# Other places in SBUF for the matmul operands of a two-block float32 network

## The chip, the cores and the metric

The kernel runs on one core of a Trainium2 chip. The metric is the device time of one execution in microseconds (us); durations of single instructions are in nanoseconds (ns). All inputs and outputs are float32.

## The reference, cut to what matters

The input is one sequence of 256 tokens of 1024 channels. A first network of two layers and a second of two layers run one after the other. Cut to its matrix products:

```python
def swiglu(h, w_gate, w_up, w_down):                     # 1024 -> 2816 -> 1024
    return (silu(h @ w_gate) * (h @ w_up)) @ w_down
# first block: swiglu, even mixer, swiglu, swiglu, odd mixer, swiglu
for layer in range(2):                                   # second block
    proj = h @ w_in[layer]                               # 1024 -> 11776
    y_a, y_b, y_c = retention(proj), hgrn(proj), window_attention(proj)
    merged = sum(sigmoid(gate_i) * (y_i @ w_i) for i in "abc")
    h = layer_norm(alpha * h + merged @ w_o[layer])
    ff = swiglu(h) if layer == 0 else moe(h)             # 8 experts of 3584, 2 per token
    h = layer_norm(alpha * h + ff)
```

The mixers hold small pieces of other work (attention, scans, spatial gates), which take little of the time.

## The kernel before, in words

**Precision.** A float32 operand is split into a high part, rounded to the TensorE's fp32r type, and the rest (`xh`, `xl` for activations, `wh`, `wl` for weights). A product is three fp32r matmuls: high by high, high by low, low by high (`mm3w`, `mm3x`). Everything goes through `mm` (L241), whose second argument is the stationary operand, loaded into the array by a weight load (PEld in the profile), and whose third is the moving operand, streamed through it. In a profile row such as `pa<-xh,wh` the moving operand stands first and the stationary one second.

**Weight stream.** `Stream` reads all weights from HBM in order, in chunks of 128 x 2048 (1 MB, 8192 bytes of each partition), into the tiles `raw` (four buffers, and seven more in the pool `extra` for the experts). Each half chunk is split: ScalarE writes `wh` (L159), VectorE writes `wl` (L160), four buffers each. The loads are issued by SyncE in order; one waits until VectorE has split the chunk that had the buffer before.

**Dense products, weights stationary.** `proj_t_steps` gives the result transposed: the stationary operand is a 128 x 128 piece of the weights (512 bytes of each partition), the moving operand 256 tokens of an activation tile (1024 bytes). Every matmul has a weight load of its own. The moving tiles are `xh`, `xl` (the normed input of each stage), `hh`, `hl` (the hidden layer of a swiglu, `ffn_core`), `oh`, `ol` (in the second block, under this name also `sh`, `hh`, `rh` and the last), and in the mixers `ah`, `gh`, `yh`, `ch` with their low parts. A swiglu runs 22 blocks of gate and up (moving `xh`, `xl`: 22 x 8 x 2 x 3 = 1056 matmuls), then four pairs of output blocks over 22 rows (moving `hh`, `hl`: 4 x 22 x 2 x 3 = 528 matmuls).

**Products with the weights moving.** `proj_x_steps` and the experts: the moving operand is 512 columns of a weight piece (2048 bytes), the stationary one 128 tokens of an activation tile. For an expert these are the gathered tokens `gxh`, `gxl` (`gate_up`) and the hidden layer `mhh`, `mhl` (`down`); expert by expert, seven blocks of 512 hidden columns, with gate and up of a block ahead of the down product of the block before. Gathering (every second expert) and scattering (each expert) are small matmuls between.

**Places in SBUF.** Pools are laid out in the order in which they are opened, tiles in a pool in the order in which they are first used, each right behind the one before. So the place of a tile follows from the sizes ahead of it. The pool `one` (`vecs2` 256 bytes, `x` 8192, the identity and the ones 512 each, `mhalf` 64, `xh` and `xl` 8192 each) begins at byte 16,512 of each partition, which is 128 in its stretch of 512 bytes. Behind it lie `raw`, `hi`, `lo` and `wk`, all multiples of 512 bytes up to `hi` and `lo`. With one stretch meaning 512 bytes, the operands start at these places in a stretch; all their slices lie whole stretches further (for `wh`, `wl`: 512 or 1024 bytes), so the place holds for each matmul:

| operand | before | after |
|---|---|---|
| `wh`, `wl` (stationary in dense products, moving in the experts) | 448 | 448 |
| `xh`, `xl` | 448 | 128 |
| `hh`, `hl` of the first swiglu, `ffn1(0, 0)` | 288 | 128 |
| `hh`, `hl` of `ffn1(0, 1)`, `ffn1(1, 0)` and `ffn2` | 0 | 128 |
| `hh`, `hl` of `ffn1(1, 1)` | 128 | 128 |
| `oh`, `ol` in `layer0` / `layer1` | 0 / 320 | 128 / 128 |
| `ah`, `gh`, `yh`, `ch` with low parts | 32, 224, 192, 192 | 128 |
| `gxh`, `gxl`, `mhh`, `mhl` (the experts' stationary operands) | 320 | 256 |
| `raw` of the pool `raw` / of `extra` | 448 / 480 | 128 / 160 |

Of the kernel before, what the change touches and what calls it, by code (L numbers as in the profile page):

```python
# [9 lines left out]
F32 = mybir.dt.float32  # L10
# [10 lines left out]
KD = D // 128  # L21
# [3 lines left out]
NE = 8  # L25
# [10 lines left out]
N_RAW, N_EXTRA = 4, 7  # L36
# [138 lines left out]
        return self.hi[q][:, o:o + w], self.lo[q][:, o:o + w]  # L175


class Net:
    def __init__(self, ctx, tc, a, consts):
        self.tc, self.nc, self.a = tc, tc.nc, a  # L180
        self.ctx = ctx
        self.cn = consts
        pool = lambda n, b, **k: ctx.enter_context(tc.tile_pool(name=n, bufs=b, **k))
        self.one = pool("one", 1)
        self.raw_p, self.hi_p, self.lo_p = pool("raw", N_RAW), pool("hi", 4), pool("lo", 4)
        self.wk = pool("wk", 2)
        self.pa = pool("pa", 4, space=PSUM)
        self.pb = pool("pb", 4, space=PSUM)
        self.ws = Stream(tc, a["dense"], (self.raw_p, self.hi_p, self.lo_p))
# [25 lines left out]
    def setup(self):  # L215
        nc = self.nc
        self.ctx1 = self.ctx.enter_context(ExitStack())
        one1 = self.ctx1.enter_context(self.tc.tile_pool(name="one1", bufs=1, reuse_waits="tile"))
        self.vecs = {v: p.tile([128, NVEC[v]], F32, name=v) for v, p in (("vecs1", one1), ("vecs2", self.one))}
        nc.scalar.dma_start(self.vecs["vecs1"], self.a["vecs1"])  # L220
        self.x = self.one.tile([128, KD, S], F32, name="x")
        self.ws.load_to(0, [lambda s=slice(2 * d, 2 * d + 2): nc.sync.dma_start(self.x[:, s], self.a["xt"][:, s])
                            for d in range(4)])
        self.ws.split_to(1)
        self.ws.load_to(1)
        self.ident = self.consts(self.one, "all")["ident"]
        nc.gpsimd.dma_start(self.vecs["vecs2"], self.a["vecs2"])
        self.ones = self.one.tile([128, 128], F32, name="ones")
        nc.vector.memset(self.ones, 1.0)
        self.mhalf = self.one.tile([128, 16], F32, name="mhalf")  # L230
        nc.vector.memset(self.mhalf, -0.5)
        self.xh = self.one.tile([128, KD, S], F32R, name="xh")
        self.xl = self.one.tile([128, KD, S], F32R, name="xl")
# [136 lines left out]
        return factors  # L370


    def ffn_core(self, gname, uname, dname, gi, di, factors, done, fill=iter(())):

        nc = self.nc
        with self.tc.tile_pool(name="ffn", bufs=1, reuse_waits="tile") as fp:
            hh = fp.tile([128, NF, S], F32R, name="hh")
            hl = fp.tile([128, NF, S], F32R, name="hl")
            proj = lambda f: self.proj_t([(gname, gi, f * 128, 128), (uname, gi, f * 128, 128)], self.xh, self.xl)
            first = []  # L380
            if factors:
                first = [proj(0), proj(1)]
                rc, R = factors()
            for f in range(NF):
                b = first.pop(0) if first else proj(f)
                sg = self.wk.tile([128, S], F32, name="sg", tag="t256", bufs=4)
                h = self.wk.tile([128, S], F32, name="h", tag="t256", bufs=4)
                if not factors:
                    nc.scalar.activation(sg, b[:, 0], AF.Silu)
                    nc.vector.tensor_mul(h, sg, b[:, 1])  # L390
                else:
                    gu = self.wk.tile([128, 2, S], F32, name="gu", tag="t512", bufs=4)
                    nc.vector.tensor_mul(gu, b, R[:, None, :].to_broadcast([128, 2, S]))
                    nc.scalar.activation(sg, gu[:, 0], AF.Silu)
                    nc.vector.tensor_mul(h, sg, gu[:, 1])
                self.split(hh[:, f], hl[:, f], h)
                if f % 3 == 2:
                    next(fill, None)
            for d in range(KD // 2):
                done(d, lambda: self.proj_t([(dname, di, d * 256, 256)], hh, hl, NF))  # L400
                next(fill, None)

    def ffn1(self, l, j, fill=iter(()), after=None):
        nc = self.nc
        factors = self.rms_in(self.vec("norm", (l * 3 + 2 * j) * 8, 8))

# [3 lines left out]
            if after:  # L410
                after(d)

        self.ffn_core("ffn_w_gate", "ffn_w_up", "ffn_w_down", (l, j), (l, j), factors, done, fill)

    def add_out(self, d, b):
        xp = self.x[:, 2 * d:2 * d + 2]
# [34 lines left out]
    def even(self):  # L451
# [5 lines left out]
        with tc.tile_pool(name="ev", bufs=1, reuse_waits="tile") as P:  # L457
# [60 lines left out]
                nc.scalar.activation(vt[:, t], o[t], AF.Copy, scale=rc[:, t:t + 1])  # L518


            ah = P.tile([128, 4, S], F32R, name="ah")
            al = P.tile([128, 4, S], F32R, name="al")
            tr = nc.tensor.transpose
# [99 lines left out]
            nc.vector.tensor_reduce(ms[:, 1], vq, axis=AX.X, op=OP.add)  # L623
            rv = self.rstd_cols(ms[:, 1], 16, 1.0 / 64, 1e-5)
            nc.vector.tensor_mul(vg, vg, rv[:, :, None].to_broadcast([128, 16, 64]))
            gh = P.tile([128, 4, S], F32R, name="gh")
            gl = P.tile([128, 4, S], F32R, name="gl")
            for i in range(2):
# [141 lines left out]
    def odd(self):  # L770
        nc, W, tc, s5 = self.nc, self.wk, self.tc, self.s5
        factors = self.rms_in(self.vec("norm", 32, 8))
        w, idx = "od_w_in", (0,)
        with tc.tile_pool(name="od", bufs=1, reuse_waits="tile") as P:
            pm = self.consts(P, "odd")["pool"]
            pw = self.load(P, "pw", [128, 4, 128], self.a["pw"])
            u = P.tile([128, 4, S], F32, name="s5u")
# [525 lines left out]

    def moe_fetch(self):

        p = self.ctx2.enter_context(self.tc.tile_pool(name="extra", bufs=N_EXTRA, side="right", reuse_waits="tile"))
        self.moe_ws = Stream(self.tc, self.a["moe"], (self.raw_p, self.hi_p, self.lo_p), extra=p)
        for c in range(N_RAW, N_RAW + N_EXTRA):
# [18 lines left out]
    def router_parts(self):  # L1327

        V = self.nc.vector
        self.wg = self.mo.tile([128, KD, NE], F32, name="wg")  # L1330
        self.wsum = self.mo.tile([128, 2, NE], F32, name="wsum")
        wr, wb = (self.wk.tile([128, KD, NE], F32, name=n, tag="t256", bufs=4) for n in ("wr", "wb"))
        self.nc.gpsimd.dma_start(wr, self.a["router"])
        b = self.pbank((128, 2, NE))
# [29 lines left out]
        self.ln_finish(self.vec("lnmix", 0, 8), self.vec("lnmix", 8, 8))  # L1364

    def ffn2(self):
        self.ffn_core("ffn_w_gate_2", "ffn_w_up_2", "ffn_w_down_2", (0,), (0,), None, self.residual2)
        self.ln_finish(self.vec("lnffn", 0, 8), self.vec("lnffn", 8, 8))

    def ln_stats(self, x):  # L1370
# [35 lines left out]
    def moe(self):  # L1406
# [2 lines left out]
        Z = self.mo  # L1409
        x = self.hx  # L1410
        C = self.consts(Z, "moe")
        cr = Z.tile([128, 2, 128], F32R, name="cr")
        V.tensor_copy(cr[:, 0], C["before"])
        V.tensor_copy(cr[:, 1], self.ones)
# [299 lines left out]
    def run(self):  # L1714
        tc = self.tc
        self.setup()
        with tc.tile_pool(name="evw", bufs=1, reuse_waits="tile") as P:
            steps = self.even_loads(P)
            self.ffn1(0, 0, steps)
            for _ in steps:  # L1720
                pass
            self.even()
        with tc.tile_pool(name="s5p", bufs=1, reuse_waits="tile") as P2:
            with tc.tile_pool(name="s5q", bufs=1, reuse_waits="tile") as P:
                steps = self.s5_params(P, P2)
                self.ffn1(0, 1, steps)
                self.ffn1(1, 0, steps)
                for _ in steps:
                    pass
            self.odd()  # L1730
# [1 line left out]
        self.ctx1.close()  # L1732
        with tc.tile_pool(name="l2", bufs=1, reuse_waits="tile") as Q:
            self.l2 = Q
            self.layer0()
        self.ffn2()
        self.run_last()

    def run_last(self):

        tc = self.tc
        with ExitStack() as self.ctx2:
            self.mo = self.ctx2.enter_context(tc.tile_pool(name="hxp", bufs=1))
            with tc.tile_pool(name="l2b", bufs=1, reuse_waits="tile") as Q:
                self.l2 = Q
                self.layer1()
            self.mo = self.ctx2.enter_context(tc.tile_pool(name="mo", bufs=1, reuse_waits="tile"))
            self.moe()
# [88 lines left out]
```

## Time and profile before

| | |
|---|---|
| median of 3 runs | 3186.09 us (3184.33 to 3187.4) |
| the profiled execution | 3184.51 us |
| its span, first to last instruction | 3182.7 us |
| TensorE (PE) busy | 97% of the span, 20841 matmuls |
| weight loads (PEld) / VectorE (DVE) / ScalarE (ACT) busy | 88% / 73% / 58% |
| mean granted TensorE clock | 0.987 of full speed |
| read from HBM | 691.92 MB |

A matmul's busy time in the profile is from its start to its modelled end, and matmuls overlap in the array; so what tells its cost is the distance from one start to the next. In the profile's time, `ffn1(0, 0)` runs to about 205 us, `ffn1(0, 1)` from 344 to 521, `ffn1(1, 0)` from 536 to 713, `ffn1(1, 1)` from 847 to 1023, `layer0` to 1475, `ffn2` to 1677, `layer1` to 2134 and the experts from about 2160 to 3166 us. PEclk is the granted TensorE clock of a stretch as a share of full speed, 2.4 GHz; the other level, 1.2 GHz, is a half.

### The profile page before, as it was taken

What the parts mean: (1) busy time and instruction counts of PE and PEld (TensorE: products, weight loads), DVE (VectorE), ACT (ScalarE), POOL (GpSimd) and SP (SyncE); (2) the same over time, 40 slices, a digit from 0 to 9 for tenths busy, and PEclk for the clock granted to TensorE, in tenths of its full rate; (3) what the DMA queues carried; (4) which work ended last, traced back from release to release, by engine and by line L of the source; (5) the groups of instructions that cost most, each with busy time, mean ns of one, the idle gap of its engine ahead of it and who ended that gap; (6) DMA issues with size and microseconds to landing.
All of it is one profiled execution on the core that took longest, in us unless ns stands there. A gap on an engine that the chain in (4) does not pass through costs nothing. (4 is left out here: it accounts for less than half of the span.)

```text
span 3182.7 us, 51831 instructions
## 1 busy us (share of the span) xinstructions
PE 3090.5 (97%) x20841; PEld 2796.7 (88%) x20841; DVE 2337.7 (73%) x3444; ACT 1852.9 (58%) x2527; POOL 186.8 (6%) x159
## 2 busy tenths in 40 slices
PE   8999999999999999999999999998999999999998
PEld 8997999996899899899998899987877878878876
DVE  6667787768765675556556765468999999999988
ACT  5456555542444664554445645456777777777775
POOL 1000000002102000102010000010000000000000
PEclk9999999999999999999999999999999999999999
DMA  6542555551455333454553335657998999999994
GB/s 247 195 158 91 179 186 179 181 200 74 159 183 191 120 120 134 169 182 154 186 178 128 121 119 171 239 215 277 363 353 331 360 352 340 358 350 340 354 360 156
DMA packets 97414, 696.37 MB, mean 219 GB/s; under 512 B 10880, under 2 KB 11232, under 8 KB 13456
## 3 DMA queue, kind: packets, MB, share of 16 engines
q1 hardware_dynamic: 95184, 685.81, 58.8%
q0 software_dynamic: 752, 3.85, 0.3%
q8 instruction: 165, 2.70, 0.3%
q10 hardware_dynamic: 1232, 3.34, 0.3%
q14 instruction: 81, 0.66, 0.1%
HBM read 691.92 MB, written 1.05 MB: 218 GB/s over the span
## 5 line engine op out<-in xcount | busy, mean ns | idle before, releaser
L160 DVE TENSOR_TENSOR wl<-raw,wh 128x1024 fp32r<-128x1024 f32 x1299 | 1583.0, 1234 | 535.5 <-ACT wh L159 527.8
L159 ACT ACTIVATE wh<-raw 128x1024 fp32r<-128x1024 f32 x1299 | 1360.3, 1058 | 842.4 <-PE pa L241 672.6
L241 PE MATMUL pa<-xh,wh 128*128 128x256 f32 x3072 | 879.2, 286 | 13.4 <-ACT wh L159 10.1
L241 PE MATMUL pa<-xl,wh 128*128 128x256 f32 x3072 | 877.2, 286 | 3.7 <-DVE xl L339 3.7
L241 PE MATMUL pa<-xh,wl 128*128 128x256 f32 x3072 | 876.7, 285 | 0.5 <-DVE wl L160 0.5
L241 PEld LDWEIGHTS pa<-xh,wh 128*128 128x128 f32 x3072 | 595.1, 194 | 17.6 <-ACT wh L159 10.1
L241 PEld LDWEIGHTS pa<-xl,wh 128*128 128x128 f32 x3072 | 594.6, 194 | 5.8 <-DVE xl L339 4.5
L241 PEld LDWEIGHTS pa<-xh,wl 128*128 128x128 f32 x3072 | 594.9, 194 | 1.1 <-DVE wl L160 0.8
L241 PE MATMUL pa<-wl,gxh 128*128 128x512 f32 x896 | 354.6, 396 | 1.3 <-DVE wl L160 1.3
L241 PE MATMUL pa<-wh,gxl 128*128 128x512 f32 x896 | 353.6, 395 | 0.0
L241 PE MATMUL pa<-wh,gxh 128*128 128x512 f32 x896 | 322.6, 395 | 0.0
L241 PE MATMUL pa<-hl,wh 128*128 128x256 f32 x880 | 246.0, 280 | 0.0
L241 PE MATMUL pa<-hh,wl 128*128 128x256 f32 x880 | 245.8, 279 | 0.0
L241 PE MATMUL pa<-hh,wh 128*128 128x256 f32 x880 | 245.6, 279 | 0.0
L241 PEld LDWEIGHTS pa<-wl,gxh 128*128 128x128 f32 x896 | 168.5, 188 | 43.8 <-DVE wl L160 3.4
L241 PEld LDWEIGHTS pa<-wh,gxh 128*128 128x128 f32 x896 | 168.6, 188 | 39.9
L241 PEld LDWEIGHTS pa<-wh,gxl 128*128 128x128 f32 x896 | 168.5, 188 | 39.2
L241 PE MATMUL pb<-wl,mhh 128*128 128x512 f32 x448 | 179.1, 400 | 0.0
L241 PE MATMUL pb<-wh,mhl 128*128 128x512 f32 x448 | 177.3, 396 | 0.0
L241 PEld LDWEIGHTS pa<-hh,wh 128*128 128x128 f32 x880 | 165.7, 188 | 0.0
L241 PEld LDWEIGHTS pa<-hh,wl 128*128 128x128 f32 x880 | 165.2, 188 | 0.1
L241 PEld LDWEIGHTS pa<-hl,wh 128*128 128x128 f32 x880 | 164.8, 187 | 0.0
(506 smaller groups left out, 4042.0 us busy)
## 6 DMA issues: line engine op xcount, KB each, us to landing
raw<-in_moe SPq DMA_DIRECT2D x336, 1024.0 KB, 5.6
raw<-in_dense SPq DMA_DIRECT2D x315, 1024.0 KB, 4.8
c_lay<-in_c_lay POOLq DMA_DIRECT2D x2, 1152.0 KB, 6.1
x<-in_xt SPq DMA_DIRECT2D x4, 256.0 KB, 6.1
raw<-in_dense SPq DMA_DIRECT2D x4, 256.0 KB, 7.0
w<-in_cw ACTq DMA_DIRECT2D x1, 1024.0 KB, 8.1
out_dram<-hx SPq DMA_DIRECT2D x2, 512.0 KB, 2.6
c_odd<-in_c_odd POOLq DMA_DIRECT2D x1, 768.0 KB, 4.6
```

Of the source, the lines that this page charges most:

```text
L159: self.nc.scalar.activation(h, src, AF.Copy)
L160: self.nc.vector.tensor_sub(l, src, h)
L241: self.nc.tensor.matmul(out, l, r, start=start, stop=stop, skip_group_check=True)
```

## The change

No instruction is added, removed or put in another place in the order. Two small tiles leave the pool `one` for a new pool `two` that lies between `raw` and `hi`, so that everything from `x` to `raw` lies 256 or 320 bytes lower and `hi` lies where it was. Unwritten tiles (`gap`) move the other operands up. The router's two small tiles leave the pool of the experts for one of their own at the far end of SBUF, which moves the pool `extra` 320 bytes down. The table above has the places that result.

```diff
+def gap(pool, n, name):
...
+    pool.tile([128, n // 4], F32, name="gap_" + name)
...
-        self.raw_p, self.hi_p, self.lo_p = pool("raw", N_RAW), pool("hi", 4), pool("lo", 4)
+        self.raw_p = pool("raw", N_RAW)
+        self.two = pool("two", 1)
+        self.hi_p, self.lo_p = pool("hi", 4), pool("lo", 4)
...
-        self.vecs = {v: p.tile([128, NVEC[v]], F32, name=v) for v, p in (("vecs1", one1), ("vecs2", self.one))}
+        self.vecs = {v: p.tile([128, NVEC[v]], F32, name=v) for v, p in (("vecs1", one1), ("vecs2", self.two))}
...
-        self.mhalf = self.one.tile([128, 16], F32, name="mhalf")
+        self.mhalf = self.two.tile([128, 16], F32, name="mhalf")
...
-    def ffn_core(self, gname, uname, dname, gi, di, factors, done, fill=iter(())):
+    def ffn_core(self, gname, uname, dname, gi, di, factors, done, fill=iter(()), free=0):
...
+            if free:
+                gap(fp, free, "h")
             hh = fp.tile([128, NF, S], F32R, name="hh")
...
+            gap(P, 96, "a")
             ah = P.tile([128, 4, S], F32R, name="ah")
...
+            gap(P, 320, "g")
             gh = P.tile([128, 4, S], F32R, name="gh")
...
+            gap(P, 448, "od")
             pm = self.consts(P, "odd")["pool"]
...
+        self.rt = self.ctx2.enter_context(self.tc.tile_pool(name="router", bufs=1, side="right"))
         p = self.ctx2.enter_context(self.tc.tile_pool(name="extra", bufs=N_EXTRA, side="right", reuse_waits="tile"))
...
-        self.wg = self.mo.tile([128, KD, NE], F32, name="wg")
-        self.wsum = self.mo.tile([128, 2, NE], F32, name="wsum")
+        self.wg = self.rt.tile([128, KD, NE], F32, name="wg")
+        self.wsum = self.rt.tile([128, 2, NE], F32, name="wsum")
...
-        self.ffn_core("ffn_w_gate_2", "ffn_w_up_2", "ffn_w_down_2", (0,), (0,), None, self.residual2)
+        self.ffn_core("ffn_w_gate_2", "ffn_w_up_2", "ffn_w_down_2", (0,), (0,), None, self.residual2, free=128)
...
         C = self.consts(Z, "moe")
+        gap(Z, 256, "mo")
...
-            self.ffn1(0, 0, steps)
+            self.ffn1(0, 0, steps, free=352)
...
-                self.ffn1(0, 1, steps)
-                self.ffn1(1, 0, steps)
+                self.ffn1(0, 1, steps, free=128)
+                self.ffn1(1, 0, steps, free=128)
...
             self.l2 = Q
+            gap(Q, 128, "l2")
             self.layer0()
...
                 self.l2 = Q
+                gap(Q, 128, "l2")
                 self.layer1()
```

## Rows read from the trace of the kernel before

**Rows 1.** The page's first part: busy time, share of span, instructions.

```profile
PE 3090.5 (97%) x20841; PEld 2796.7 (88%) x20841; DVE 2337.7 (73%) x3444; ACT 1852.9 (58%) x2527; POOL 186.8 (6%) x159
```

**Rows 2.** Windows: length, each engine's busy us and instructions, PEclk, DMA, GB/s.

```profile
850.00:962.00 112.00, 112.00 (x935) 112.00 (x935) 74.94 (x101) 54.70 (x82) 0.00 (x0) 1.00 0.51 181
962.00:1024.00 62.00, 61.93 (x541) 61.58 (x540) 38.13 (x37) 27.60 (x31) 15.28 (x11) 1.00 0.53 187
1024.00:1480.00 456.00, 441.97 (x3385) 417.85 (x3384) 277.98 (x550) 239.38 (x379) 42.69 (x47) 0.98 0.42 150
2500.00:2700.00 200.00, 197.86 (x886) 159.61 (x885) 180.63 (x175) 151.49 (x167) 0.00 (x0) 1.00 0.92 348
```

**Rows 3.** Waits of SyncE's DMA queue: waited for, us, times, longest.

```profile
SPq L142 <- DVE wl L160: 2280.4, 538, 42.9
```

**Rows 4.** Timeline of PE at the start, ten matmuls from first to last.

```profile
12.13 0.41 PE L241 MATMUL pa<-xh,wl 128*128 128x256 f32 x1
...
14.05 0.41 PE L241 MATMUL pa<-xh,wl 128*128 128x256 f32 x1
```

**Rows 5.** Windows of PE at L241: length, busy us (matmuls), PEclk, DMA, GB/s.

```profile
850.00:960.00 110.00, 110.00 (x919) 1.00 0.51 179
142.00:202.00 60.00, 60.00 (x502) 1.00 0.50 176
462.00:520.00 58.00, 58.00 (x494) 1.00 0.52 189
963.00:979.00 16.00, 16.00 (x143) 1.00 0.54 198
982.00:1022.00 40.00, 40.00 (x356) 1.00 0.54 186
```

**Rows 6.** Timeline of PE: first and last of three stretches of 48 matmuls.

```profile
1299.42 0.40 PE L241 MATMUL pa<-wh,xh 128*128 128x512 f32 x1
...
1310.10 0.39 PE L241 MATMUL pa<-wh,xl 128*128 128x512 f32 x1
...
1342.70 0.28 PE L241 MATMUL pa<-oh,wh 128*128 128x256 f32 x1
...
1348.24 0.28 PE L241 MATMUL pa<-oh,wl 128*128 128x256 f32 x1
...
2209.72 0.39 PE L241 MATMUL pa<-wh,gxh 128*128 128x512 f32 x1
...
2220.64 0.39 PE L241 MATMUL pa<-wh,gxl 128*128 128x512 f32 x1
```

**Rows 7.** Groups of PE matmuls by tile and form: count, busy us, mean ns.

```profile
L241 PE MATMUL pa<-xh,wh 128*128 128x256 f32 x3072 | 879.2, 286 | 13.4 <-ACT wh L159 10.1 <-ACT xh L982 3.3
...
L241 PE MATMUL pa<-wh,gxh 128*128 128x512 f32 x896 | 322.6, 395 | 0.0
...
L241 PE MATMUL pa<-hl,wh 128*128 128x256 f32 x880 | 246.0, 280 | 0.0
...
L241 PE MATMUL pb<-wh,mhh 128*128 128x512 f32 x448 | 163.8, 396 | 0.0
...
L241 PE MATMUL pa<-oh,wh 128*128 128x256 f32 x448 | 126.2, 282 | 0.0
...
L241 PE MATMUL pa<-ch,wh 128*128 128x256 f32 x64 | 18.4, 290 | 0.0
```

**Rows 8.** Group of VectorE's splits; DMA sums, 2160 to 3100 us; busiest windows.

```profile
L160 DVE TENSOR_TENSOR wl<-raw,wh 128x1024 fp32r<-128x1024 f32 x1299 | 1583.0, 1234 | 535.5 <-ACT wh L159 527.8 <-DMA raw<-in_moe 2.1
...
DMA packets 44860, 327.02 MB, mean 348 GB/s; under 512 B 4976, under 2 KB 4976, under 8 KB 4976
...
raw<-in_moe SPq DMA_DIRECT2D x312, 1024.0 KB, 5.5
...
2680.00:2700.00 20.00, 19.15 (x84) 14.98 (x83) 19.21 (x19) 14.15 (x15) 0.00 (x0) 1.00 0.84 308
2760.00:2780.00 20.00, 20.00 (x91) 16.26 (x91) 18.03 (x17) 15.35 (x17) 0.00 (x0) 1.00 0.96 376
```

More of the change, by code (lines that the diff above doesn't have):

```diff
@@ L401, in ffn_core, with ffn1 @@
                 next(fill, None)
-    def ffn1(self, l, j, fill=iter(()), after=None):
+    def ffn1(self, l, j, fill=iter(()), after=None, free=0):
         nc = self.nc
@@ L411, in done @@
                 after(d)
-        self.ffn_core("ffn_w_gate", "ffn_w_up", "ffn_w_down", (l, j), (l, j), factors, done, fill)
+        self.ffn_core("ffn_w_gate", "ffn_w_up", "ffn_w_down", (l, j), (l, j), factors, done, fill, free)
     def add_out(self, d, b):
```

## The prediction

> **What bounds the kernel now.** I read the page's busy shares first, then windows by stage, then waits, and last the distances from one matmul to the next. TensorE is busy 97% of the span [rows 1], and in the dense stages it is busy without a gap: 112.00 of 112 us in the gate and up part of a swiglu, 61.93 of 62 in its down part, 442 of 456 in the first mixer stage of the second block, with VectorE at 61 to 67% and the DMA engines near half [rows 2]. In the experts it is busy 197.86 of 200 us, with VectorE at 180.63 (90%) and DMA at 92% [rows 2]. SyncE's loads wait for buffers (2280 us on VectorE's splits), so the weights are fetched as far ahead as the ring allows [rows 3]. So the end is set by how fast TensorE takes one matmul after the other, and since a busy TensorE says nothing of its pace, the distances decide.
>
> At the start TensorE runs at 1.2 GHz, and nine distances take 1.92 us: 213.3 ns for 256 columns, which is just 256 cycles [rows 4]. At 2.4 GHz the same would be 106.7 ns. Later rows are at PEclk 1.00, so each ns above 106.7 is lost between matmuls. A window also counts the matmul that hangs over its edge (0.28 us each), so I divide its length plus 0.28 by its count. With the weights at place 448 in all of them [rows 5]:
>
> - moving operand at 448 (`xh`): 110.28 / 919 = 120.0 ns;
> - at 288 (`hh`, first swiglu): 60.28 / 502 = 120.1 ns;
> - at 0 (`hh`, second swiglu): 58.28 / 494 = 118.0 ns;
> - at 128 (`hh` of `ffn1(1, 1)`, by chance already there): (16.28 + 40.28) / (143 + 356) = 113.4 ns.
>
> The second and fourth are the same loop with the same shapes and weight buffers. `oh` at 0 gives 5.54 / 47 = 117.9 ns [rows 6]. So the trace of before holds the new geometry of every dense product in one stage, and there the pace is 6.6 ns better than for `xh`.
>
> For 512 columns: stationary `xh` at 448 under weights at 448 takes 10.68 / 47 = 227.2 ns; the experts' `gxh` at 320 under weights at 448 takes 10.92 / 47 = 232.3 ns [rows 6]. Against 213.3 ns (512 cycles at 2.4 GHz) the losses are 13.9 and 19.0.
>
> **The change, part by part.** *Dense products, weights stationary.* All moving operands go to 128 and I price all at 113.4 ns. The counts are of [rows 7], each group three times (high by high, high by low, low by high). `xh`: 9216 x 6.6 = 60.8 us. `hh`: of 2640, 528 stay as they are, 528 gain 6.7 (3.5 us), and 1584 gain 4.6 (7.3 us). `oh`: 1344 x 4.5, at the rate of place 0 (the half that lies at 320 is taken alike) = 6.0. `ch` 192, and by the loops 96 each of `ah`, `gh`, `yh`, taken at 4.5: 2.2. Sum 79.8 us. Against it: where TensorE waits for a chain on other engines, a faster matmul only lengthens the wait. In the windows of [rows 2] it idles 0 to 3%, so I keep 76 of the 79.8. Nothing else is near: VectorE would go from 67% to 71% in the gate and up part, and DMA moved 186 to 198 GB/s at the faster pace in the down part [rows 5], half of what it moves in the experts.
>
> A rule of the Trainium skill speaks against this part. The windows above show 120.0 against 113.4 ns with nothing different but the place of the moving operand. "TensorE: Matmul & The Clock Gate", section "Step-by-step: what each phase is for", says that TensorE reads the moving operand and the weight load through two independent ports, so that loading the next weights takes nothing from the running matmul. By the rule places would not matter and this part would be worth 0; by the rows it is worth 76 us. The rows here disagree with it, so I go by them.
>
> *Experts.* Moving weights stay at 448, stationary operands go from 320 to 256. No row shows 512 columns at this distance, so the price is bounded. What the rows share is the distance from the stationary to the moving place, modulo 512: 0 costs 13.3 ns with 256 columns and 13.9 with 512, so the loss seems to belong to the one weight load per matmul and not to the columns. At 128 - 448, that is 192, it is 6.7 with 256 columns. The experts come to 448 - 256 = 192 too, from 128. Below, the loss can't go under 0 (213.3 ns); above, the worst in these rows is the present 232.3. I take the row of the same distance, 213.3 + 6.7 = 220.0. The experts have 3 x 896 + 3 x 448 = 4032 such matmuls [rows 7], so 12.3 x 4032 = 49.6 us (bounds 0 and 77).
>
> What comes next there is VectorE, at 90.3% [rows 2]: `wl` takes 1234 ns for each half chunk [rows 8]. With 50 us less in the 940 from 2160 to 3100, the same work is 90.3% x 940 / 890 = 95.4%. A window with 19.21 of 20 us shows that it can run at 96% while TensorE is busy 19.15 [rows 8], but with less slack for bursts. DMA would have to move 327 MB in 890 us, 367 GB/s; a window of 20 us has 376, and a load lands 5.5 us after its issue while eleven buffers turn [rows 8]. So both just suffice. I take 45 of the 49.6.
>
> *All else.* The products with stationary `xh` under moving weights go from distance 0 to 320, and the small fp32 products (transposes, attention, scans), the gather and the scatter shift as well, about 3100 matmuls in all (20841 less the groups above). Nothing shows their price; the spread of the other places (118.0 to 120.1) bounds it at 2 ns either way, 6 us, and 6.6 ns if some land on the good distance, 20 us. I take 0. VectorE, ScalarE and DMA read and write at other places too; if `wl` lost as much as a matmul does, 13 of 1234 ns, VectorE would be 1% busier, which the slack above covers. The gap tiles are never written, so they issue no instruction and no transfer; they can only shift which earlier tile a later one lies on. The loads in the changed order stay in SyncE's queue in the same order.
>
> Sum: 76 + 45 = 121 us. From the profiled execution, 3184.5 - 121 = 3063.5. The median of the runs shown is 1.6 us above it, which gives 3065 us.
>
> **Rivals.**
>
> *The experts gain little.* For it: the distance to the good place was seen with the moving operand shifted and with 256 columns alone, and in the experts three engines run within 10% of each other. Against it: the agreement of 13.3 and 13.9. With 0 to 20 us from the experts and 76 from the rest, the time is 3090 to 3110 us.
>
> *The dense gain comes only in part.* The mixers may be held by their chains, or the gain at 128 may need the `hh` tiles' spacing. Then `ffn` stages alone gain, which have five times 1056 `xh` and the `hh` products: 35 + 11 = 46 us, and the experts little: about 3140.
>
> *Nothing changes.* Places are not what matters, and `ffn1(1, 1)` was faster for another reason: its `fill` steps are empty. By this the time stays at 3186. The port rule cited above would give the same. Against it: the neighbouring gate and up part of the same call runs at 120.0, and VectorE and ScalarE, which fill steps load, are not what TensorE waits for. An allocation that comes out otherwise than the sizes say would give this too.
>
> *Slower.* The experts' matmuls get worse at the new distance instead of better. Distances 0 and 128 cost 13.9 and 19.0; if the trend went on, 192 would cost more still. The dense 76 us are used up when each of the 4032 loses 76 / 4032 = 19 ns more, a pace of 251 ns; no row comes near. At that point and beyond the time is over 3186, at 255 ns some 3200.
>
> **How the numbers follow.** Forecast as summed, dense near 76 and experts 25 or more (3040 to 3090): 0.60. Experts little (3090 to 3115): 0.24. Dense in part (3115 to 3175): 0.07. Nothing: 0.05. Slower: 0.04. The predicted time is 3065. The range must leave out no more than 0.2: down to 3040 (80 us dense and 66 in the experts, a pace of 216 ns), up to 3115 (76 dense less 5 of the unpriced rest, experts 0). That holds about 0.82. What a measurement of this kernel can tell from no change is about 0.2%, or 6 us: faster 0.91, within it 0.05, slower 0.04.
>
> **What the changed profile would show.** The gate and up part of each swiglu at 113.4 ns, 22 x 48 matmuls in about 120 us and not 127; the down parts of all swiglus alike; the `gxh` groups near 220 ns with VectorE at 95%. Wrong for the dense part: `xh` still at 118 or more at PEclk 1.00. Wrong for the experts: a distance over 228 ns, or 220 ns with new waits of TensorE on `wl`. The prediction fails as a whole if the pace hangs on something that `ffn1(1, 1)` has alone.

## The result, and the profile after

| | median | lowest to highest | profiled execution |
|---|---|---|---|
| before | 3185.21 us | 3183.53 to 3187.4 | 3184.51 us |
| after | 3137.4 us | 3128.5 to 3142.22 (4 executions) | 3141.89 us, span 3140.1 |

The ratio is 0.9846, interval [0.9819, 0.9873]: the change saves 1.5%, 48 us between the medians and 42.6 between the profiled executions. Forecast were 121 us, so 3137 lies above the range of 3040 to 3115. In two series of the experiments below one execution each ran at a mean granted clock of 0.69 and 0.78 of full speed (4062 and 3642 us); they are left out of the numbers given.

The page's first part for the kernel after, to set beside [rows 1]; `mm` is L250 here:

```profile
PE 3046.8 (97%) x20841; PEld 2748.4 (88%) x20841; DVE 2341.3 (75%) x3444; ACT 1855.7 (59%) x2527; POOL 187.2 (6%) x159
```

TensorE's busy time falls by 43.7 us, from 3090.5, and its share stays at 97%: the gain is all in the pace, not in waits. So I read the pace as in [rows 5], length plus 0.28 us by count. First the gate and up parts of the five swiglus (windows of TensorE at the line of `mm`: length, busy us and matmuls, PEclk, DMA, GB/s):

```profile
40.00:130.00 90.00, 90.00 (x797) 1.00 0.63 224
340.00:440.00 100.00, 100.00 (x851) 1.00 0.54 191
530.00:630.00 100.00, 100.00 (x851) 1.00 0.52 190
840.00:940.00 100.00, 100.00 (x852) 1.00 0.52 184
1470.00:1570.00 100.00, 100.00 (x885) 1.00 0.57 200
```

That is 113.3, 117.8, 117.8, 117.7 and 113.3 ns, where before all stood at 120.0 as in the first of [rows 5]. The five run the same loop with the same tiles at the same places, and yet there are two paces. The down parts of the first four, with `hh`:

```profile
140.00:190.00 50.00, 50.00 (x443) 1.00 0.57 198
450.00:500.00 50.00, 50.00 (x427) 1.00 0.50 176
640.00:690.00 50.00, 50.00 (x427) 1.00 0.52 178
944.00:960.00 16.00, 16.00 (x138) 1.00 0.58 198
965.00:1000.00 35.00, 35.00 (x311) 1.00 0.52 181
```

These are 113.5, 117.8 and 117.8 ns, and the last two rows are one stage, `ffn1(1, 1)`: 118.0 and then 113.4, with a few small products on `ones` between them. A pace holds over hundreds of matmuls and changes where the stream is interrupted. Below, 113.3 (up to 113.5) is called the fast pace and 117.8 (117.6 to 118.0) the slow one.

In the experts, a stretch of 48 (timeline of TensorE, first and last) and a window as in [rows 2]:

```profile
2217.06 0.40 PE L250 MATMUL pa<-wh,gxh 128*128 128x512 f32 x1
...
2228.03 0.40 PE L250 MATMUL pa<-wh,gxl 128*128 128x512 f32 x1
```

```profile
2500.00:2700.00 200.00, 197.87 (x888) 159.44 (x887) 180.58 (x178) 151.13 (x165) 0.00 (x0) 1.00 0.91 349
```

10.97 / 47 = 233.4 ns against 232.3 in [rows 6]. 888 matmuls in 200 us against 886, VectorE at 90% as before, no new wait: the experts are as they were, or about 1 ns a matmul worse. From the first matmul on `gxh` to the end of the last on `mhl` they take 1006.9 us in the trace of before and 1009.3 in that of after.

Distance below is the moving operand's place less the stationary one's, modulo 512, in bytes. The dense products moved to distance 192, the experts from 128 to 192.

### The profile page after: what moved, and what is told of

Its sections match the earlier page's. It is cut to its first block, busy times and chain, and to the rows that moved or that the text cites. A ratio compares the mean times of both kernels' runs of the same rounds, so it can differ in the third digit from the quotient of the medians.

```text
span 3140.1 us, 51830 instructions
## 1 busy us (share of the span) xinstructions
PE 3046.8 (97%) x20841; PEld 2748.4 (88%) x20841; DVE 2341.3 (75%) x3444; ACT 1855.7 (59%) x2527; POOL 187.2 (6%) x159
## 5 line engine op out<-in xcount | busy, mean ns | idle before, releaser
L250 PE MATMUL pa<-xh,wh 128*128 128x256 f32 x3072 | 867.5, 283 | 13.2 <-ACT wh L159 9.8
L250 PE MATMUL pa<-xl,wh 128*128 128x256 f32 x3072 | 865.4, 282 | 4.1 <-DVE xl L348 3.9
L250 PE MATMUL pa<-xh,wl 128*128 128x256 f32 x3072 | 864.2, 281 | 0.5 <-DVE wl L160 0.5
L250 PEld LDWEIGHTS pa<-xh,wh 128*128 128x128 f32 x3072 | 585.5, 191 | 17.3 <-ACT wh L159 9.8
L250 PEld LDWEIGHTS pa<-xl,wh 128*128 128x128 f32 x3072 | 584.2, 190 | 6.6 <-DVE xl L348 5.3
L250 PEld LDWEIGHTS pa<-xh,wl 128*128 128x128 f32 x3072 | 587.3, 191 | 1.1 <-DVE wl L160 0.8
L250 PE MATMUL pa<-wl,gxh 128*128 128x512 f32 x896 | 354.6, 396 | 1.3 <-DVE wl L160 1.3
L250 PE MATMUL pa<-wh,gxl 128*128 128x512 f32 x896 | 354.2, 395 | 0.0
L250 PE MATMUL pa<-wh,gxh 128*128 128x512 f32 x896 | 323.2, 395 | 0.0
L250 PE MATMUL pa<-hh,wl 128*128 128x256 f32 x880 | 246.0, 280 | 0.0
L250 PE MATMUL pa<-hl,wh 128*128 128x256 f32 x880 | 245.9, 279 | 0.0
L250 PE MATMUL pa<-hh,wh 128*128 128x256 f32 x880 | 245.8, 279 | 0.0
L250 PEld LDWEIGHTS pa<-wl,gxh 128*128 128x128 f32 x896 | 168.4, 188 | 43.9 <-DVE wl L160 3.4
L250 PEld LDWEIGHTS pa<-wh,gxh 128*128 128x128 f32 x896 | 168.4, 188 | 40.7
L250 PEld LDWEIGHTS pa<-wh,gxl 128*128 128x128 f32 x896 | 168.3, 188 | 40.5
L250 PE MATMUL pb<-wl,mhh 128*128 128x512 f32 x448 | 179.2, 400 | 0.0
L250 PE MATMUL pb<-wh,mhl 128*128 128x512 f32 x448 | 177.8, 397 | 0.0
L250 PEld LDWEIGHTS pa<-hh,wl 128*128 128x128 f32 x880 | 167.3, 190 | 0.1
L250 PEld LDWEIGHTS pa<-hh,wh 128*128 128x128 f32 x880 | 165.5, 188 | 0.0
L250 PEld LDWEIGHTS pa<-hl,wh 128*128 128x128 f32 x880 | 165.2, 188 | 0.0
```

Source lines behind the costliest of these rows:

```text
L250: self.nc.tensor.matmul(out, l, r, start=start, stop=stop, skip_group_check=True)
```

## The experiments

Times are device us beside the kernel before on the same chip (medians 3184.2 to 3185.5 in all series). A "stretch of twelve" is twelve matmuls of one form in a row, read from their starts.

### One part alone: `experts_part`

```diff
 # kernel before, plus only:
+        self.rt = self.ctx2.enter_context(self.tc.tile_pool(name="router", bufs=1, side="right"))
-        self.wg = self.mo.tile(...)       # and wsum
+        self.wg = self.rt.tile(...)
         C = self.consts(Z, "moe")
+        gap(Z, 256, "mo")
```

> The kernel before with the experts' part of the change alone: their stationary operands go from 320 to 256 (distance 128 to 192), all else stays. By the prediction's price (220.0 ns) the time falls by 45 us to about 3140. By the pace seen in the kernel after (233.3 ns and no slack to lose) it does not fall: 0 to 5 us more, 3185 to 3190 us.

Measured: 3186.21 (3183.04 to 3191.27, 10 executions), ratio 1.0005 [0.9996, 1.0014]. A stretch of its experts:

```profile
2210.30 0.40 PE L245 MATMUL pa<-wh,gxh 128*128 128x512 f32 x1
...
2221.27 0.39 PE L245 MATMUL pa<-wh,gxl 128*128 128x512 f32 x1
```

10.97 / 47 = 233.4 ns. The experts' part of the change is worth nothing, at best 1 us, at worst a loss of 4.5. So 45 us of the forecast fall away here, and the whole gain is the dense part's.

This trace shows one thing more. Its dense part is that of before, instruction for instruction and place for place, so it is a second look at the one stage from which the prediction took 113.4 ns, the down part of `ffn1(1, 1)` (windows as in the last two of [rows 5]):

```profile
963.00:979.00 16.00, 16.00 (x144) 1.00 0.56 198
982.00:1022.00 40.00, 40.00 (x342) 1.00 0.51 175
```

The first window gives 113.1 ns, the second 40.28 / 342 = 117.8, where before had 113.2 with 356 matmuls. The second pace was there with the old places too.

### The same kernel again: `again`

No edit.

> The changed kernel as it is. Two-pace theory: with the moving operand at 128 and the weights at 448 a stream of dense matmuls runs at either 113.3 or 117.9 ns, the pace is taken when the stream restarts after other work and held to the next such break, so which stage has which pace differs from execution to execution. Then at least one of the five gate-up parts (in the first profile of the changed kernel 113.3, 117.9, 117.9, 117.9, 113.3) has another pace here, and the executions scatter over 10 us or more (before: 4 us). Stage theory: the pace belongs to the stage (its place in the weight stream, its buffers); the five parts repeat their paces and the executions scatter no more than before. Experts: 233 ns in both.

Measured: 3130.5 (3127.1 to 3133.48), ratio 0.9823 [0.9807, 0.984]. The windows of its five gate and up parts:

```profile
40.00:130.00 90.00, 90.00 (x797) 1.00 0.63 223
350.00:440.00 90.00, 90.00 (x796) 1.00 0.55 192
550.00:640.00 90.00, 90.00 (x767) 1.00 0.53 188
870.00:960.00 90.00, 89.93 (x787) 1.00 0.54 195
1500.00:1570.00 70.00, 70.00 (x621) 1.00 0.54 195
```

113.3, 113.4, 117.7 and, in the last, 113.2; the fourth window reaches past the end of its part, whose blocks ran at 113.3. The second and fourth parts were at 117.8 in the first profile. So the pace belongs neither to a stage nor to its places: one and the same program, with the same instructions in the same order, comes out either way. The four executions lie within 6.4 us, not the 10 or more that were expected; with the four of the first series they span 15. Of the stretches of twelve at distance 192, 533 were fast and 461 slow in the first profile (75 lay across a break), 734 and 263 in this one. Some 200 stretches less are slow: 200 x 12 x 4.45 ns = 10.7 us, and the spans differ by 10.4 (3140.1 to 3129.7).

### Other places and other distances: `elsewhere`, `scan`, `fine`

```diff
 # elsewhere: pool "one" and all behind it 160 bytes up, so xh lies at 288 and wh at 96
 # (four small tiles lose a second buffer to make the room)
+        gap(self.one, 160, "first")
 # elsewhere / scan: a distance of its own for hh in each swiglu
-            self.ffn1(0, 0, steps, free=352)
+            self.ffn1(0, 0, steps, free=64)      # scan: 384
 ...
-        gap(Z, 256, "mo")
+        gap(Z, 352, "mo")                        # scan: 448; and a gap ahead of mhh
 # fine: hh starts some elements into a longer tile
+            hh, hl = (fp.tile([128, NF * S + 128], F32R, name=n)[:, e:e + NF * S]...
```

> xh at 288 and the weights at 96: both 160 bytes further, the distance of 192 kept. If the distance alone counts, xh shows the same two paces, 113.3 and 117.9, and no other. If the place itself counts (128 and 448), xh shows something else, 118 to 120 as the other places of before did. The hidden tiles of the five swiglus lie at distances 256, 288, 320, 384, 416 in this order, a scan without a forecast for each: if distance 192 is special they show 117 to 121 and never 113.3. Experts: gxh at distance 256 and mhh at 320; if the distance counts with 512 columns they differ from 233, at 320 near the 229 that the last product of layer1 had at that distance; if places do not matter to the experts, 232 to 233 for both.

> xh as in the changed kernel (113.3 or 117.9 by stretch). The hidden tiles of the five swiglus lie at distances 224, 32, 96, 128, 160 in this order; if 192 is special, none runs at 113.3; if there is a stretch of good distances around it, 160 and 224 do too. Experts: gxh at distance 0, mhh at 64. By the distance theory gxh runs at the 227.2 ns that xh as the stationary operand had at distance 0 before, 5 to 6 ns less than 233, some 15 us off the gate-up part of the experts; if the experts' pace is set by something else than places, 232 to 233.

> The hidden tiles of the five swiglus at distances 176, 184, 196, 200, 208 in this order, between the steps of 32 of before: if the fast pace belongs to a narrow range of distances around 192, some of these run at 113.3 in all blocks and some at 117 to 118; if only at 192 exactly, none does. Experts: gxh at distance 160 and mhh at 224; with the period of 256 bytes that the scan showed (0 and 256 both 226.7, 64 and 320 both 229), they are the two that are still unknown; no forecast but that they lie between 226.7 and 233.3.

Measured, one execution each: 3116.53, 3123.33 and 3152.49. The windows of the first gate and up part and of the first three down parts of `elsewhere` (`hh` at distances 256, 288, 320):

```profile
40.00:130.00 90.00, 90.00 (x796) 1.00 0.63 224
142.00:195.00 53.00, 53.00 (x444) 1.00 0.51 181
455.00:505.00 50.00, 50.00 (x431) 1.00 0.53 186
640.00:690.00 50.00, 50.00 (x427) 1.00 0.56 203
```

The first three down parts of `scan` (distances 224, 32, 96):

```profile
142.00:195.00 53.00, 53.00 (x450) 1.00 0.53 193
455.00:505.00 50.00, 50.00 (x431) 1.00 0.54 189
640.00:690.00 50.00, 50.00 (x419) 1.00 0.53 188
```

And of `fine` (176, 184, 196):

```profile
142.00:195.00 53.00, 53.00 (x446) 1.00 0.52 182
455.00:505.00 50.00, 50.00 (x419) 1.00 0.50 182
640.00:690.00 50.00, 50.00 (x419) 1.00 0.55 190
```

Pairs of distances 256 apart agree where both were tried, so they share a column (ns, median of the stretches of twelve; before included):

| 256 columns, distance | 0, 256 | 32, 288 | 64, 320 | 96, 352 | 128, 384 | 160, 416 | 176 | 184 | 192 | 196, 200 | 208 | 224 |
|---|---|---|---|---|---|---|---|---|---|---|---|---|
| pace | 120.0 | 116.7 | 117.8 | 120.0 | 120.0 | 117.4 | 119.2 | 120.0 | 113.3 or 117.8 | 120.0 | 119.0 | 118.3 |

| 512 columns, distance | 0, 256 | 64, 320 | 128 | 160 | 32, 192 |
|---|---|---|---|---|---|
| pace | 226.7 | 229.0 | 232.4 to 232.9 | 234.3 | 233.3 |

Three things follow. With both operands 160 bytes higher, `xh` keeps its paces (113.4 in the first row of `elsewhere`, where all five parts were fast), and `hh` has the same pace at distances 288 and 32, 256 apart (116.7), with the weights at 96 and at 448, so the distance counts and not the place. Distance 192 is the only one that gives 113.3 through whole stages; 4 bytes beside it (196) the pace is 120.0. And with 512 columns the order is another one: 0 is best, and 192, the best for 256 columns, is among the worst.

But the medians hide that a distance other than 192 can have two paces as well. In before, `oh` at distance 64 has 117.9 in [rows 6] and 117.7 or 117.8 in most other streams, and yet one stream without interruption goes like this:

```profile
1195.25 0.28 PE L241 MATMUL pa<-oh,wh 128*128 128x256 f32 x1
...
1200.23 0.28 PE L241 MATMUL pa<-oh,wl 128*128 128x256 f32 x1
```

4.98 / 44 = 113.2 ns. `oh` at distance 384 has 118.7 in before (`layer1`), 117.7 in `experts_part`, and `hh` there has 120.0 in `elsewhere`. With 512 columns and stationary `oh` at distance 320, the last product of `layer1` has 228.6 ns in after and 233.4 in `scan`, where the operands lie at the same places (22.17 / 95):

```profile
2069.42 0.40 PE L250 MATMUL pa<-wh,oh 128*128 128x512 f32 x1
...
2091.59 0.39 PE L250 MATMUL pa<-wh,ol 128*128 128x512 f32 x1
```

So an entry seen in one or two streams need not be the only pace of its distance.

### What changes the pace: `poke`, `poke_twice`

```diff
             for f in range(NF):
+                if not first:      # poke_twice: this matmul two times
+                    self.mm(self.pbank((128, 2))[:, 0:1], self.ones, self.ones[:, 0:1], True, True)
                 b = first.pop(0) if first else proj(f)
```

The experts of `poke` lie at distances 32 (gate and up) and 96 (down), those of `poke_twice` at 0.

> One extra matmul of a single column (its result is not used) ahead of each of 102 gate-up blocks, the rest of the dense part as in the changed kernel. Two-pace theory: each block of 48 matmuls takes its pace anew, so blocks of 113.3 and of 117.9 alternate within one swiglu, with changes at the extra matmuls and nowhere else. Stage theory: every swiglu keeps one pace through all its blocks. The extra matmuls cost 0.1 to 0.3 us each, 10 to 30 us. Experts: gxh at distance 32 and mhh at 96, by the distance theory different from 233, by the other 232 to 233.

> The kernel after with two small float32 matmuls instead of one ahead of each gate and up block, and the experts at distance 0. If each small matmul toggles a state with two values, two of them leave it: all blocks of a swiglu hold one pace, 113.3 or 117.8 ns, with no change from block to block. If a restart picks its pace anew, the blocks change without order; if any interruption toggles once however long it is, they alternate as with one small matmul. Time 3150 to 3180 us either way (102 more small matmuls at about 0.2 us, 18 us less in the experts than with one small matmul).

Measured, one execution each: 3161.9 and 3190.81. Two successive blocks of `poke` (timeline of TensorE; one small float32 matmul makes the row with x2):

```profile
65.22 0.28 PE L250 MATMUL pb<-ones 128*128 128x1 f32 x2
...
65.57 0.28 PE L250 MATMUL pa<-xl,wh 128*128 128x256 f32 x1
...
70.80 0.28 PE L250 MATMUL pa<-xh,wl 128*128 128x256 f32 x1
70.91 0.28 PE L250 MATMUL pb<-ones 128*128 128x1 f32 x2
...
71.25 0.28 PE L250 MATMUL pa<-xl,wh 128*128 128x256 f32 x1
...
76.67 0.28 PE L250 MATMUL pa<-xh,wl 128*128 128x256 f32 x1
```

From the second matmul of a block to its last are 46 distances: 5.23 / 46 = 113.7 ns, then 5.42 / 46 = 117.8. So it goes on: of the 76 pairs of neighbouring blocks with nothing else between them, 36 went from fast to slow, 40 from slow to fast, none kept its pace. These pairs lie in the first four swiglus. In the fifth the small matmuls stand together at its start, with none between the blocks, and all 22 blocks keep one pace (113.3 in `poke`, 117.8 in `poke_twice`), but for the first matmuls, 213 ns apart. In `poke_twice` all 76 second blocks were slow, 74 behind a slow one and 2 behind a fast one. The 74 fit a state that two small matmuls toggle and toggle back; only the 2 speak against it, and for two small matmuls setting the slow pace. Its time lies above the 3150 to 3180 us expected. A small change in TensorE's own stream thus changes the pace at once, while the surroundings (DMA, splits) don't alternate with the blocks. But the order of the instructions isn't all: it is the same in `after` and `again`, whose paces differ, so something in the moments at which a stream starts again counts too. No run here isolates it.

### The experts at distance 0: `experts0`

```diff
-        gap(Z, 256, "mo")
+        gap(Z, 448, "mo")
```

> The changed kernel with one number different: the experts' stationary operands at 448, distance 0 to the moving weights, not 256, distance 192. Distance theory: 226.7 ns for 233.3, 4032 x 6.6 = 27 us less than the changed kernel, 3103 to 3112 us. Rival, another engine bounds the experts: TensorE then waits on VectorE's splits and less than 10 us of it is seen.

Measured: 3118.89 (3104.45 to 3125.71, 5 executions), ratio 0.9801 [0.9784, 0.9817]. A stretch of the experts, and the window at their middle:

```profile
2222.42 0.39 PE L250 MATMUL pa<-wh,gxh 128*128 128x512 f32 x1
...
2233.07 0.39 PE L250 MATMUL pa<-wh,gxl 128*128 128x512 f32 x1
```

```profile
2500.00:2700.00 200.00, 199.12 (x916) 164.85 (x915) 184.18 (x180) 157.41 (x172) 0.00 (x0) 1.00 0.94 358
```

10.65 / 47 = 226.6 ns, and 916 matmuls in 200 us against 888. At 6.7 ns a matmul 4032 of them give 27 us at most. The stage itself, measured as above, takes 986.6 us against 1009.3 in after and 1009.6 in `again`: 23 us less. The profiled spans of this kernel and of `again` differ by 27.1, the medians by 11.6, with executions that scatter over 21 and 6 us, and the median lies above the 3103 to 3112 expected. The paces of the dense part can explain that (a gate and up part at the slow pace costs 1056 x 4.45 ns = 4.7 us); only one execution of each has a trace. VectorE doesn't stand in the way: at the higher pace it is 92% busy, with TensorE at 199.12 of 200.

### Setting the pace: six spare matmuls

```diff
     # proj_t_steps, once after self.settle was set
+            if self.settle:
+                self.settle = False
+                spare = self.pbank((128, 2, S))
+                for n in range(6):
+                    self.mm(spare[:, n % 2], wh[:, 0:128], wl, n == 0, n == 5)   # distance 0
     # settle32, poke_settle32, settle_mid: distance 32 instead
+                    ... self.xh.rearrange("p k s -> p (k s)")[:, 88:344] ...
     # settle, settle32: set where the gate and up blocks start again behind the wait for the norm,
     # and at the start of some mixer parts (12 places, 72 matmuls); settle_mid, settle_mid0: one block later
+                if f == (3 if factors else 1):
+                    self.settle = True
     # poke_settle, poke_settle32: ahead of each block, behind the small float32 matmul
```

All have the experts at distance 0.

> The changed kernel with six extra matmuls at distance 0 only where a long stretch begins (each swiglu's gate-up part, the down part after its first block where other work breaks it, each gate of the second block), 0.7 us each, some 13 of them, 9 us; experts at distance 0. Settling theory: all five gate-up parts at 113.3, some 10,000 matmuls of which about 40% ran at 117.8 before, so 18 us gained against 9 paid, and 4032 x 6.7 = 27 us from the experts: about 3095 to 3105 us and a scatter of few us. Alternation theory: paces scattered as before, 3110 to 3120.

> As poke, and behind each of the 102 extra matmuls six more of 256 columns with the weights both stationary and moving, which is distance 0 (results not used); experts at distance 0. Settling theory: a stretch at another distance leaves the array always in the same relation of weight loads to matmuls, from which distance 192 falls into the fast pace; so after the six every block runs at 113.3 ns, where poke alternated 113.3 and 117.8 block by block. Alternation theory: the six change nothing or add a fixed step, and the blocks alternate or all run at 117.8. Cost of the extras 102 x (0.25 + 0.72) = some 100 us, so about 3190 us less 20 for the experts.

> The kernel after with the experts at distance 0 and six spare matmuls at distance 32 at 13 restarts (start of the gate and up blocks of each swiglu and mixer stages). If distance 32 forces the fast pace: all five gate and up parts at 113.3 ns and nearly no execution above 3112 us, median 3103 to 3110. If the pace is left to chance, one or two parts of five run at 117.8 ns and executions scatter from 3105 to 3130 us, median near 3120.

> The kernel after with one small float32 matmul and six spare matmuls at distance 32 ahead of each gate and up block, the experts at distance 0 (the same with distance 0 in place of 32 held 117.8 ns through two of four stages with pokes). If a stretch at distance 32 puts the next one at distance 192 into its fast pace, all gate and up blocks run at 113.3 ns in all five swiglus: about 3195 to 3205 us. If it does nothing, some swiglus hold 117.8 ns as with distance 0 (3205 to 3225 us) or alternate.

> As the kernel with six spare matmuls at distance 32 at 13 restarts, but in the swiglus they come one block after the wait, in the middle of a stream. If a stretch at distance 32 in the stream sets the fast pace: all five gate and up parts at 113.3 ns from there on, whatever the block before ran at; some 9 us less than with two slow gate and up parts, so a median of 3104 to 3112 us. If the pace is left to chance: one or two of five parts at 117.8 ns, the block before and the one behind agree, and a median of 3113 to 3120 us.

> The same places for the six spare matmuls, at distance 0. If any stretch at another distance in the stream sets the fast pace, as with distance 32: five of five fast, 3104 to 3112 us. If distance 0 leaves the pace as it was (with a small float32 matmul ahead of it, it did so 95 times of 95): parts that start at 117.8 ns stay there, 3112 to 3125 us.

| kernel | distance, where | us, lowest to highest | ratio | gate and up parts fast |
|---|---|---|---|---|
| `settle` | 0, behind the wait | 3106.87 to 3114.3 (3) | 0.9765 [0.9745, 0.9785] | 5 of 5 |
| `settle32` | 32, behind the wait | 3111.32 to 3118.3 (5) | 0.9782 [0.9769, 0.9795] | 3 of 5 |
| `settle_mid` | 32, one block later | 3107.29 to 3119.36 (5) | 0.9781 [0.9767, 0.9796] | 4 of 5 |
| `settle_mid0` | 0, one block later | 3097.69 to 3104.52 (5) | 0.9736 [0.9723, 0.9749] | 5 of 5 |
| `poke_settle` | 0, behind each small matmul | 3214.72 (1) | | 3 of 5 |
| `poke_settle32` | 32, behind each small matmul | 3197.4 (1) | | 5 of 5 |

All five gate and up parts of `settle_mid0`, at 113.4 ns, and the last of `settle_mid`, at 117.9:

```profile
40.00:130.00 90.00, 90.00 (x796) 1.00 0.61 224
345.00:435.00 90.00, 90.00 (x796) 1.00 0.54 192
530.00:620.00 90.00, 90.00 (x797) 1.00 0.55 199
830.00:920.00 90.00, 90.00 (x796) 1.00 0.54 194
1470.00:1560.00 90.00, 90.00 (x796) 1.00 0.54 192
```

```profile
1470.00:1560.00 90.00, 90.00 (x766) 1.00 0.52 186
```

The times of `settle` and `poke_settle` lie above those expected (3095 to 3105, some 3170). The median of `settle_mid` (3117.4) lies where chance was to put it, that of `settle_mid0` (3103.34) just below the range for five fast parts.

The expectation for distance 32 failed: in `settle32` two parts were slow, and in `settle_mid`, with the six matmuls in the middle of the stream, two stretches that had begun slow stayed so (in `settle32` one went from slow to fast). With distance 0 the ten parts of `settle` and `settle_mid0` were fast, which shows little by itself: in four of the five parts of `settle_mid0` the stream was fast already ahead of the six, and in the six kernels in which nothing was done about it (`after`, `again`, `elsewhere`, `scan`, `fine`, `experts0`) 23 of 30 parts were fast, so that ten of ten come by luck in 7% of all cases (0.77 to the tenth). More telling are the places where the six stood in a stream without a wait: 3 streams went from slow to fast, 9 stayed fast, none got or stayed slow. All 3 pass from `oh` to `xh` at the six, and without them such a stream keeps its pace: so it did at all 175 passages between `oh` and `xh` of five kernels (`after`, `again`, `scan`, `fine`, `experts0`), 58 of them slow. One of the 3, in `settle_mid0` (timeline, then a window of TensorE behind the six), and last the window at the same point of `settle_mid`:

```profile
1848.75 0.28 PE L251 MATMUL pa<-oh,wh 128*128 128x256 f32 x1
...
1854.29 0.28 PE L251 MATMUL pa<-oh,wl 128*128 128x256 f32 x1
1854.40 0.88 PE L251 MATMUL pb<-wl,wh 128*128 128x256 f32 x6
```

```profile
1856.00:1871.00 15.00, 15.00 (x134) 1.00 0.58 204
```

```profile
1861.00:1876.00 15.00, 15.00 (x130) 1.00 0.56 199
```

5.54 / 47 = 117.9 ns ahead of the six, 15.28 / 134 = 114.0 behind them; in `settle_mid`, with distance 32, the stream stays slow at 117.5. The times agree: five executions of `settle_mid0` lie between 3097.7 and 3104.5, five of `experts0` between 3104.45 and 3125.7, which differs from it by these 72 matmuls only, and the interval lies wholly below that of `settle_mid`, which differs by the distance of the six alone.

The rule is still not whole. In `poke_settle`, with a small float32 matmul right ahead of the six, 57 fast blocks stayed fast and 38 slow ones stayed slow: the windows of its first two parts give 114.0 and 117.5 ns with the small and the spare matmuls counted in, and no block between changed.

```profile
60.00:140.00 80.00, 80.00 (x704) 1.00 0.52 184
390.00:440.00 50.00, 50.00 (x428) 1.00 0.45 164
```

So six matmuls at distance 0 don't set the fast pace from every state. In `poke_settle32` all 96 pairs were fast behind fast, which tells nothing of what a slow one would have done.

`settle_mid0` is the best version: 3103.34 us, 2.6% below before and 1.1% below after.

## Why the prediction was wrong

**What bounds the kernel** was right: TensorE's pace. The gain came as shorter distances between matmuls with TensorE busy to 97% before and after, and places alone moved it. The rival that nothing changes is out: the same instructions run at 113.3 to 120.0 ns, and the distance of the two operands has a part in it. With it goes the port rule of the Trainium skill ("TensorE: Matmul & The Clock Gate", section "Step-by-step: what each phase is for") as a rule on the time of this case; no run here shows whether the ports are where that time goes.

**Dense products: the step "I price all at 113.4 ns" failed.** It took one stage of before, with 499 matmuls in two windows, for the pace of a place. Distance 192 has two paces, and that stage happened to show the fast one twice; in `experts_part`, with the same dense part, most of the same stage ran at 117.8. That the price came out as 113.4 was luck of one profiled execution. The trace of before held a warning, the stream of `oh` at 113.2 among others of the same form and places at 117.8. In the profile of after, 331 of 691 stretches of twelve `xh` matmuls gained 6.7 ns, 311 gained 2.2, and 49 lay across a break: 9216 x (331 x 6.7 + 311 x 2.2) / 691 = 39 us instead of 60.8. Only the 2.2 ns of the slow pace are sure, an estimate of 20 us.

The distances between starts, added up over the whole traces of before and after, leave nothing out: `xh` took 39.6 us less, `oh` 5.2, `hh` 3.2 (nearly all in the first swiglu; elsewhere the slow pace equals that of the old places, 117.8 against 118.0; 10.8 were forecast), and `ah`, `gh`, `yh`, `ch` 2.1. Of these 50.1 us the experts took back 2.5, longer waits between `xh` matmuls 3.3 (the 3.8 that the prediction set aside for them was well judged), and all the rest 1.8, which makes the 42.6 measured. The last sentence of the prediction named the danger, that the pace hangs on something which `ffn1(1, 1)` has alone. It hung on something that the places don't fix, and that this stage didn't always have either. The prediction took the shift of pace by place from rows at several places, but the price at the new place from a single stage, and gave its range no room for a second pace.

**Experts: the step "I take the row of the same distance, 220.0 ns" failed.** The distance does decide, as `elsewhere` shows, but the price doesn't carry from 256 columns to 512. The agreement at distance 0 (13.3 and 13.9 ns above 106.7 and 213.3) was one pair, and doesn't hold elsewhere: at 192 the losses are 6.7 or 11.1 with 256 columns and 20.0 with 512. The upper bound, "the worst in these rows is the present 232.3", was passed by 1 ns. Of the 45 us forecast nothing came, as `experts_part` shows by itself. The prediction's own rows held the better choice: stationary `xh` at distance 0 under 512 columns took 227.2 ns in [rows 6], and the experts at distance 0 take 226.7.

**Rivals.** "The experts gain little" was right on its point, with 0 as its lower end, but built on a full dense gain. "The dense gain comes only in part" gives 3140, which is near, but for another reason: it would have left the mixers without gain, and they ran at the same two paces as the swiglus. So its nearness is no merit of its mechanism. "Nothing changes" was right in one point, that `ffn1(1, 1)` was fast for a reason beside its place, though the empty `fill` steps weren't it: in `experts_part` they are empty too. "Slower" had the right trend for the experts (0 better than 128, 192 worse still) and rightly asked for 19 ns, of which 1 came.

**All else at 0** held: the rest named above comes to 1.8 us, and VectorE's busy time went from 2337.7 to 2341.3.

What stays open: what in the hardware makes these paces, why they repeat with 256 bytes of distance, why 512 columns prefer other distances, and by which rule what stands ahead picks one of two paces. The experiments show only that a change in TensorE's stream changes the choice, and that within a stream without interruption it holds.

## What to carry to other kernels

Where TensorE is busy without gaps and every matmul has its own weight load, read the distance between starts, not the busy share, and try the operands' distance as a parameter, for each form by itself: here 113.3 to 120.0 ns and 226.7 to 234.3 ns. Before a pace from one stretch prices thousands of instructions, look for a second stretch of the same geometry, in another stage and another execution; one stretch can't show that there are two paces, and a second profile of the kernel before would have shown it here. A price found with one size isn't carried to another by a rule that fits at a single point.

## What the hardware showed that I had not expected

- Two paces of one form at one geometry, 113.3 and 117.8 ns, held for whole stages and changed at interruptions of TensorE's stream; executions of one program differ by them (3128.5 to 3142.22 us, where before has 3183.53 to 3187.4).
- A single matmul of one column ahead of a block turned the pace over 76 times of 76; behind two of them the block was slow 76 times of 76, 74 of them behind a slow one.
- Two paces aren't bound to distance 192 or to 256 columns: `oh` at distance 64 ran at 113.2 and 117.8 in before, and 512 columns at distance 320 at 228.6 and 233.4.
- At PEclk 1.00, which is 2.4 GHz, 113.3 and 120.0 ns are 272 and 288 cycles, 16 and 32 above the 256 columns, and 226.7 and 233.3 ns are 544 and 560, 32 and 48 above 512. Of the paces between, 116.7 is a mixture: the single distances in the trace are 113 to 114, 116 to 118 and 120 ns. 117.8 isn't, nearly all of its distances are 117 to 119.
- A distance of 4 bytes more (192 to 196) costs 2.2 to 6.7 ns a matmul.
